# A conditioning shift summed from columns alone, six of its sixteen tiles by GpSimd and ScalarE

## The chip, the cores and the metric

The kernel runs on one core of one Trainium2 chip. The metric is the device time of one execution in microseconds. A core has five engines with a queue each, worked off in order: TensorE (PE in the profile; PEld is its weight load), VectorE (DVE), ScalarE (ACT), GpSimd (POOL) and SyncE (SP), which here only issues DMAs. Engines wait for one another through semaphores.

## The reference, cut to what matters

Two layers; each has a token mixer (a convolution module in layer 0, attention in layer 1) and then a gated network with a width-3 convolution. Every sub-layer takes its shift, scale and gate from one conditioning vector `c`:

```python
def ada_ln(c, w, b):
    mod = jax.nn.silu(c) @ w + b
    shift, scale, gate = jnp.split(mod, 3, axis=-1)
    return shift[:, None, :], scale[:, None, :], gate[:, None, :]
...
        shift, scale, gate = ada_ln(c, ffn_mod_w[i], ffn_mod_b[i])
        h = rms_norm(x, ffn_norm_g[i]) * (1.0 + scale) + shift
        x = x + gate * conv_ffn(h, ffn_up_w[i], ffn_dw_w[i], ffn_dw_b[i], ffn_down_w[i])
```

The width is 2048, the sequence 256, the network's inner width 5632. The case is about `shift` of the first network (`ffn0`): 2048 sums of 2048 products, 16 MB of weights that are read once.

## The kernel before, in words

Activations lie transposed: 16 tiles `x` of 128 channels by 256 tokens. A weight matrix is streamed in pieces of 128x1024, eight 128x128 blocks each. Except in the first product, a piece is split into two parts for exact fp32 products: ScalarE casts it to `wh` (L243), VectorE subtracts to get `wl` (L247), and TensorE multiplies both. There are four buffers of `wh` and of `wl`, six of the loaded `raw`.

A conditioning sum can be made in two ways.

- **By rows, on TensorE** (`mod_rows`, L591): 128x2048 of the weights, four matmuls of 128x512 with the conditioning vector as the stationary side. Four such steps make 512 channels; the result is turned into columns by small matmuls (L607), and a bias is added (L613).
- **By columns, on VectorE** (`mod_reduce`, L338): the transposed weights of 128 channels, 128x2048, are multiplied with the conditioning vector `csr` (a copy in each partition) and summed in one instruction, in place; L342 adds the bias at the end.

For `ffn0` the scale is made by rows (16 steps). Of the shift, `ROWS = 2` groups of 512 channels are made by rows (8 steps), and the other eight tiles by columns.

The place is the second product of the convolution module, called `pw2` here: 16 output tiles, 256 blocks, 32 pieces of weights. Its first eight output tiles are made together (L304 to L306), the last eight one after the other, two pieces each (L298, L299). Each output tile is taken out of PSUM by ScalarE (L978) and VectorE (L979, for the last eight also L981) into `x`; then ScalarE squares it (L406), GpSimd adds the square to `sumsq` (L410), and ScalarE and VectorE make the raw input of the next product (L462, L463). When the shift is complete, its two parts are written beside that input (L473, L474). After `pw2` comes the network's first up-projection, `up00a`.

Work that is not tied to a place stands in `fill`; `tick` takes one step of it after each piece of weights. `mods0` is the generator that makes the rows and the columns of `ffn0`. The framework then orders each engine's instructions; in `mods0`, `behind` keeps a sum behind the instruction that was the engine's last when it was written.

Of the kernel before, what the change touches and what calls it, by code (L numbers as in the profile page):

```python
# [10 lines left out]
F32 = mybir.dt.float32  # L11
F32R = mybir.dt.float32r
AF = mybir.ActivationFunctionType
ALU = mybir.AluOpType
PSUM = bass.MemoryType.PSUM

P = 128
# [14 lines left out]
M0 = 6  # L32
MORE_ROWS = 4
SPLIT_ROWS = 3
ROWS = 2

ROWS_AT = {**{c: (11,) for c in (2, 4, 6, 8, 10, 12)}, 13: (16, 17), 14: (8, 12, 16), 15: (2, 13, 15, 17)}
ROWS_TAIL = 5
# [2 lines left out]
         "o": (0.45, -3.0), "up00a": (0.0, 0.0), "qk0a": (0.0, 0.0),  # L41
         "up00b": (0.28, 0.0), "up10a": (0.0, 0.0), "up10b": (0.25, -2.0), "v0": (0.0, 0.0), "qk0b": (0.42, -1.5)}
QUIET = 6
PRIORITY = 100
MORE_MODS = 2

# [12 lines left out]
class Cfg:  # L59
    def __init__(self, D, T, H, F, CW, FW):  # L60
# [3 lines left out]
        self.GH = 4  # L64
        self.rows0 = min(ROWS, KD // 4)

# [52 lines left out]
def hybrid_trunk(ctx: ExitStack, tc: tile.TileContext, cfg: Cfg, io: dict):  # L119
    nc = tc.nc  # L120
    D, T, H = cfg.D, cfg.T, cfg.H
    KD, KF, CW, FW = cfg.KD, cfg.KF, cfg.CW, cfg.FW
# [34 lines left out]
    csr = const.tile([P, D], F32, name="csr")  # L157
# [10 lines left out]
    def pc(name, i0=0, n=None):  # L168
        if name in cfg.ccols:
            t, (a, b) = cpar["t"], cfg.ccols[name]  # L170
        else:
            t, (a, b) = par, cfg.cols[name]
        return t[:, a:b] if n is None else t[:, a + i0:a + i0 + n]
# [32 lines left out]
    def last_of(engine):  # L206
        return next(ins for ins in reversed(list(nc.cur_bb.bb.instructions)) if ins.engine == engine)

    def behind(ins):

        tc.add_manual_dep(list(nc.cur_bb.bb.instructions)[-1], ins.name,
                          mybir.DependencyInfo(mybir.DependencyClass.NoSync, mybir.DependencyReason.DATA),
                          reason="behind")

    def drain(gens):
        while gens:
            advance(gens, 1)
# [6 lines left out]
    def load(src, dst):  # L224
        tc.keep_in_program_order(nc.sync.dma_start(dst, src))
# [44 lines left out]
    def gemm(name, xh, xl, done, after=None, width=None, halves=0, ready=None, quiet=0,  # L270
# [10 lines left out]
        for blocks, wh, wl in pieces(name):  # L281
            for b, (nb, kt) in enumerate(blocks):
# [25 lines left out]
                if left[nb] == 0:  # L308
                    with tc.high_priority(offset=PRIORITY):
                        done(nb, ps[nb])  # L310
# [7 lines left out]
    mt_at = {"mix0": list(range(2 * KD)), "ffn0": list(range(4 * cfg.rows0, KD)) + list(range(2 * KD, 3 * KD))}  # L318
# [4 lines left out]
    macc = const.tile([P, 3 * KD], F32, name="macc")  # L323
    moda, have, shift_ready = {}, set(), {}

    def mod_load(m, nb, own=False, pool=None):

        v = (pool or mpool).tile([P, D], F32, name="mraw")
        src = io["mt_" + m][mt_at[m].index(nb) if m in mt_at else nb]
        if own:  # L330
            nc.gpsimd.dma_start(v, src)  # L331
        else:
            load(src, v)
        return v

    def mod_reduce(m, nb, v):

        nc.vector.tensor_tensor_reduce(out=v, in0=v, in1=csr, scale=1.0, scalar=0.0, op0=ALU.mult, op1=ALU.add,  # L338
                                       accum_out=macc[:, nb:nb + 1])

    def mod_sum(m, nb, n):
        nc.vector.tensor_tensor(modv[m][:, nb:nb + n], macc[:, nb:nb + n], pc(bname[m], nb, n), op=ALU.add)  # L342
# [37 lines left out]
    def halved(pool, kind, name):  # L380

        low, size, ahead = PAIRS[kind]
        at = ahead if foremost.setdefault(kind, name) == name else 0
        v = pool.tile([P, at + size], F32R, name=name)
        v = bass.AP(tensor=v.tensor, offset=v.offset + at, ap=[list(v.ap[0]), [low, 2], [1, T]])
        return v[:, 0], v[:, 1], v
# [31 lines left out]
    def act_tables(name):  # L418
        tc.keep_in_program_order(nc.scalar.preload_act_table_set(name))
# [25 lines left out]
    class Entry:  # L445
# [31 lines left out]
        def product(self, name, done, table=None):  # L477
# [4 lines left out]
            def after():  # L482
# [6 lines left out]
                if self.rs is not None:  # L489
                    free = KD if i * PB >= n else min(i * PB // FIRST, max(0, KD - STAGGER))  # L490
                    with tc.high_priority(offset=PRIORITY if i * PB >= n else 0):
                        for kt in range(len(self.h), free):
# [17 lines left out]
    with ExitStack() as cv:  # L510
        cpool = cv.enter_context(tc.tile_pool(name="conv", bufs=1))
# [34 lines left out]
        row_tiles, nrow = [], {"n": 0, "near": sum(map(len, ROWS_AT.values())) + ROWS_TAIL, "bias": False}  # L546
# [73 lines left out]
                yield  # L620

        def mods0():
            first = 4 * cfg.rows0
            todo, loaded = list(range(first, KD)), []

            def reduce_loaded():
                while loaded:
                    on = last_of(nc.vector.engine)
                    mod_reduce("ffn0", *loaded.pop(0))
                    behind(on)  # L630

            def load_one():
                nb = todo.pop(0)
                loaded.append((nb, mod_load("ffn0", nb)))

            for _ in mod_rows():
                reduce_loaded()
                yield
                if ("ffn0", 1) in have and todo:
                    load_one()  # L640
                    yield
            while todo:
                load_one()
                yield
                reduce_loaded()
            reduce_loaded()
            if first < KD:
                mod_sum("ffn0", first, KD - first)
            have.add(("ffn0", 0))
            yield  # L650

        gb = cpool.tile([P, KD], F32, name="gb")
        ready = {"k": 0}
        ys = [cpool.tile([P, T], F32, name=f"y{j}") for j in range(KD)]
        for kt in range(KD):
            nc.gpsimd.tensor_tensor(ys[kt], xs[kt], rs, op=ALU.mult)
        htiles = [h_tiles(kt) for kt in range(KD)]
# [165 lines left out]
        for i in range(KD * HEAD // PB):  # L823
            pw1_piece(next(pw1))
            if (i + 1) % (HEAD // PB) == 0:
                start_tile()
        fill.append(mods0())
        load_rows(1)
        look["load"], look["split"] = 5, 0
# [24 lines left out]
        for c in range(KD + 1):  # L854
# [6 lines left out]
            if c > 0:  # L861
                old = [(c - 1, k) for k in vector_taps(c - 1)[split(c - 1):]]
                n = max(len(taps), len(old))
                pad = lambda v: v + [None] * (n - len(v))
                taps = [t for pair in zip(pad(taps), pad(old)) for t in pair if t]
            made = 0
            for s in range(nd):
# [10 lines left out]
                if c == 0 and s % 2 == 1 and 2 + s // 2 < NH:  # L878
                    j = 2 + s // 2
# [112 lines left out]
    def ffn(i, entry, out):  # L992
# [3 lines left out]
        with ExitStack() as fs:  # L996
# [34 lines left out]
            def down_done(h):  # L1031
                def done(nb, ps):
                    if nb < KD - 2:
                        t = t256()
                        nc.scalar.activation(t, ps[:, T:2 * T], AF.Copy, scale=gate(m, nb))  # L1035
                        nc.gpsimd.tensor_tensor(xs[nb], xs[nb], t, op=ALU.add)  # L1036
                    elif nb not in LAST:
                        nc.vector.scalar_tensor_tensor(xs[nb], ps[:, T:2 * T], gate(m, nb), xs[nb],
                                                       op0=ALU.mult, op1=ALU.add)
                    nc.vector.scalar_tensor_tensor(xs[nb], ps[:, :T], gate(m, nb), xs[nb],  # L1040
                                                   op0=ALU.mult, op1=ALU.add)
                    if h == 1 and i == 0:
                        out.add(nb)
                    elif h == 1:
                        out.add(xs[nb])
                        nc.scalar.activation(xs[nb], xs[nb], AF.Copy, scale=pc("fin_g", nb, 1))
                return done
# [9 lines left out]
            act_tables("sqrt_and_others")  # L1057
            gemm(f"down{i}1", gh, gl, down_done(1), quiet=QUIET, both=gb, apart=LAST)
            drain(fill)
# [41 lines left out]
    with ExitStack() as at:  # L1101
# [12 lines left out]
        def attention(h):  # L1114
# [21 lines left out]
            yield  # L1136
            with tc.high_priority(offset=PRIORITY):
                nc.scalar.copy(mh, mk)
# [20 lines left out]
            oh[h], ol[h], ob[h] = halved(apool, "o", f"o{h}")  # L1159
            with tc.high_priority(offset=PRIORITY):  # L1160
                nc.scalar.copy(oh[h], op[:, :T])
# [64 lines left out]
        act_tables("sqrt_and_others")  # L1226
        gemm("o", oh, ol, o_done, ready=lambda kt: oh[kt] is not None, quiet=QUIET, both=ob)

# [11 lines left out]
    for h in range(2):  # L1240
        t = slice(h * HT, (h + 1) * HT)
        nc.vector.reciprocal(rs[:, t], std[:, t])
        v = mpool.tile([P, D], F32, name="mraw")[:, :KD * HT].rearrange("p (k t) -> p k t", k=KD)
# [105 lines left out]
def build(nc, cfg, arrays):  # L1349
    io = {k: nc.dram_tensor(f"in_{k}", v.shape, F32, kind="ExternalInput").ap() for k, v in arrays.items()}  # L1350
    io["out"] = nc.dram_tensor("out_0", (cfg.KD // 2, P, 2 * cfg.T), F32, kind="ExternalOutput").ap()
    with tile.TileContext(nc) as tc:
        hybrid_trunk(tc, cfg, io)
# [19 lines left out]
```

## Time and profile before

| | |
|---|---|
| median of 3 runs | 2252.18 us (2250.47 to 2254.69) |
| the profiled execution | 2246.79 us, its span 2245.1 us |
| PE busy | 2213.9 us, 99% |
| DVE busy | 1811.5 us, 81% |
| ACT busy | 1243.0 us, 55% |
| POOL busy | 417.9 us, 19% |
| DMA | 602.98 MB, mean 269 GB/s |

In rows of the profile, `out<-in` are the program's names, L338 a line of the program, xN a count; behind the bar stand busy time and mean duration, then the idle time of that engine just before these instructions and what ended it. In a timeline the first two columns are start and duration in microseconds.

### The profile page before, as it was taken

The page shows a single profiled execution, that of the slowest core. Times are in us where ns is not written, and L with a number is a line of the kernel's source. Part 1 is how long each engine was busy: PE and PEld are TensorE (multiplying, and loading weights), DVE is VectorE, ACT ScalarE, POOL GpSimd, SP SyncE. Part 2 cuts the span into 40 slices and gives each one's busy share as a digit, 9 for nine tenths or more (in the row PEclk, how much of TensorE's full clock was granted, in tenths as well). Part 3 has the DMA queues.
Part 4 walks back from the last instruction along what each step waited for, and adds up shares of the span by engine and source line. Part 5 has one row for each costly group of instructions (what it writes and reads, how often), then busy time and mean ns, then how long its engine had stood idle before and what let it go on. Part 6 is the DMA issues. An engine that isn't in the chain of part 4 may idle for free.

```text
span 2245.1 us, 35029 instructions
## 1 busy us (share of the span) xinstructions
PE 2213.9 (99%) x12994; PEld 1924.3 (86%) x12994; DVE 1811.5 (81%) x2606; ACT 1243.0 (55%) x2014; POOL 417.9 (19%) x535
## 2 busy tenths in 40 slices
PE   7999999999999999999999999999999999999997
PEld 5887677988888988888898888889888889888887
DVE  7689968989997799998876878899899755777654
ACT  2055655765554455565565555657655544655553
POOL 5058702200002100002311312222000010000031
PEclk9999999999999999999999999999999999999999
DMA  9988698778878977887656788676788656656653
GB/s 398 422 335 310 265 370 338 299 259 300 306 289 291 322 285 289 317 302 268 225 185 249 287 298 296 245 263 234 250 290 289 198 192 194 194 192 191 197 194 113
DMA packets 139134, 602.98 MB, mean 269 GB/s; under 512 B 15441, under 2 KB 15569, under 8 KB 115153
## 3 DMA queue, kind: packets, MB, share of 16 engines
q1 hardware_dynamic: 120242, 464.42, 58.3%
q0 software_dynamic: 18720, 136.32, 16.3%
q8 instruction: 102, 1.67, 0.3%
q14 instruction: 70, 0.57, 0.1%
HBM read 598.58 MB, written 2.10 MB: 268 GB/s over the span
## 4 chain that ended last, share of the span: by engine, by line
PE 87%; DVE 6%; DMA 4%; issue 2%; ACT 1%; POOL 0%; DVEq 0%; SPq 0%; ACTq 0%; POOLq 0%
PE ps L298 46%; PE ps L299 23%; PE ps L700 5%; DMA mraw<-in_mt_mix 3%; DVE mraw L338 2%; PE ps L304 2%; PE ps L306 2%; PE ps L305 1%; DVE wl L247 1%; PE ps L1198 1%; PE ps L1197 1%; PE ps L1196 1%; PE ps L591 1%; PE auxa L591 1%; DVE h L463 1%
## 5 line engine op out<-in xcount | busy, mean ns | idle before, releaser
L298 PE MATMUL ps<-h,wh 128*128 128x512 f32 x3072 | 1048.9, 390 | 0.0
L247 DVE TENSOR_TENSOR wl<-raw,wh 128x1024 fp32r<-128x1024 f32 x688 | 843.7, 1233 | 226.8 <-ACT wh L243 226.3
L243 ACT CAST wh<-raw 128x1024 fp32r<-128x1024 f32 x688 | 719.8, 1049 | 540.0 <-PE ps L298 323.1
L299 PE MATMUL ps<-h,wl 128*128 128x256 f32 x3072 | 848.3, 276 | 0.0
L298 PEld LDWEIGHTS ps<-h,wh 128*128 128x128 f32 x3072 | 576.7, 188 | 119.6
L299 PEld LDWEIGHTS ps<-h,wl 128*128 128x128 f32 x3072 | 576.7, 188 | 0.2
L298 PE MATMUL ps<-g,wh 128*128 128x512 f32 x1320 | 449.0, 389 | 0.0
L338 DVE CUSTOM_DVE_ANT_0 mraw<-mraw,csr 128x2048 f32<-128x2048 f32 x152 | 348.8, 2295 | 27.5 <-DMA mraw<-in_mt_mix 26.9
L299 PE MATMUL ps<-g,wl 128*128 128x256 f32 x1320 | 364.3, 276 | 0.0
L298 PEld LDWEIGHTS ps<-g,wh 128*128 128x128 f32 x1320 | 247.7, 188 | 51.3
L299 PEld LDWEIGHTS ps<-g,wl 128*128 128x128 f32 x1320 | 247.7, 188 | 0.0
L1014 DVE SCALAR_TENSOR_TENSOR t<-t,par 128x254 f32<-128x254 f32 x352 | 169.2, 481 | 60.6 <-ACT t L1011 55.9
L700 PE MATMUL ps<-h,raw 128*128 128x256 f32 x832 | 188.6, 381 | 0.0
L700 PEld LDWEIGHTS ps<-h,raw 128*128 128x128 f32 x832 | 157.8, 191 | 28.3 <-issue 5.8
L1011 ACT ACTIVATE t<-t,par 128x256 f32<-128x256 f32 x176 | 105.6, 600 | 132.3 <-DVE t L1008 132.1
L1036 POOL TENSOR_TENSOR x<-x,t 128x256 f32<-128x256 f32 x56 | 61.1, 1092 | 542.8 <-ACT t L1035 542.8
L740 DVE SCALAR_TENSOR_TENSOR auxb<-u,cpar,auxb 128x256 f32<-128x256 f32 x297 | 121.6, 482 | 4.5 <-ACT auxb L724 3.8
L875 POOL TENSOR_TENSOR y<-y,h 128x256 f32<-128x256 f32 x143 | 104.4, 730 | 13.4 <-ACT h L749 3.3
L331 POOL DMA_DIRECT2D mraw<-in_mt_ffn x64 | 34.5, 540 | 359.9 <-DVE t L1008 247.8
L410 POOL TENSOR_TENSOR sumsq<-sumsq,t 128x256 f32<-128x256 f32 x56 | 62.0, 1107 | 143.7 <-ACT t L406 143.6
L298 PE MATMUL ps<-o,wh 128*128 128x512 f32 x256 | 88.1, 391 | 0.0
L331 POOL DMA_DIRECT2D mraw<-in_mt_mix x48 | 25.9, 541 | 323.5 <-DVE t L1008 169.8
(259 smaller groups left out, 2525.2 us busy)
## 6 DMA issues: line engine op xcount, KB each, us to landing
raw<-in_w_down SPq DMA_DIRECT2D x176, 512.0 KB, 4.3
mraw<-in_mt_ffn POOLq DMA_DIRECT2D x64, 1024.0 KB, 5.9
raw<-in_w_pw SPq DMA_DIRECT2D x96, 512.0 KB, 7.8
mraw<-in_mt_mix POOLq DMA_DIRECT2D x48, 1024.0 KB, 5.5
raw<-in_w_up01b SPq DMA_DIRECT2D x84, 512.0 KB, 5.1
raw<-in_w_up11b SPq DMA_DIRECT2D x84, 512.0 KB, 3.7
raw<-in_w_up00b SPq DMA_DIRECT2D x80, 512.0 KB, 5.0
raw<-in_w_up10b SPq DMA_DIRECT2D x80, 512.0 KB, 4.9
```

The source lines that it names most:

```text
L243: nc.scalar.copy(wh[:, :n], v[:, :n])
L247: nc.vector.tensor_tensor(wl[:, :n], v[:, :n], wh[:, :n].bitcast(F32), op=ALU.subtract)
L298: nc.tensor.matmul(o, wh[:, c], both[kt], start=first, stop=False, skip_group_check=True)
L299: nc.tensor.matmul(o[:, :T], wl[:, c], xh[kt], start=False, stop=left[nb] == 0, skip_group_check=True)
L338: nc.vector.tensor_tensor_reduce(out=v, in0=v, in1=csr, scale=1.0, scalar=0.0, op0=ALU.mult, op1=ALU.add, accum_out=macc[:, nb:nb + 1])
L410: engine.tensor_tensor(self.sum, self.sum, sq, op=ALU.add)
L700: nc.tensor.matmul(banks[j][:, nb // KD * T:(nb // KD + 1) * T], w[:, b * P:(b + 1) * P], hf[kt], start=first, stop=left[j] == 0, skip_gro ...
L740: nc.vector.scalar_tensor_tensor(conv_ps[j], us[j % UBUFS][:, k:k + T], tap(j, k), conv_ps[j], op0=ALU.mult, op1=ALU.add)
L875: nc.gpsimd.tensor_tensor(ys[c], ys[c], pr, op=ALU.add)
L1011: nc.scalar.activation(y, ps[:, :T], AF.Identity, bias=pc(f"fdb{i}", nb, 1), scale=w(FW - 1))
L1014: nc.vector.scalar_tensor_tensor(y[:, s:], ps[:, :T - s], w(k), y[:, s:], op0=ALU.mult, op1=ALU.add)
L1036: nc.gpsimd.tensor_tensor(xs[nb], xs[nb], t, op=ALU.add)
```

## The change

All 16 tiles of the shift are summed from columns; the eight row steps, their copy, turn and bias go. The ten tiles 1, 3, 5, 7, 9, 11 and 12 to 15 are summed by VectorE as before (L338, now L339). The six tiles 0, 2, 4, 6, 8, 10 are loaded into the place of the convolution's result `y`, 16 tiles of 128x256 that are now one tile `yall` and give two buffers of 128x2048; GpSimd multiplies them with `csr` in place (L643), and three steps later ScalarE copies them onto themselves with an accumulated sum into `macc` (L657). Their loads come from SyncE's queue. The columns start when all rows have been loaded, one tile a step. Outside this the line numbers of the changed kernel are one higher up to `mods0` and 28 higher behind it (L981 is L1009).

```diff
-ROWS = 2
+ROWS = 0
+POOL_SUMS, POOL_LAG = 6, 3
...
         def mods0():
-            first = 4 * cfg.rows0
-            todo, loaded = list(range(first, KD)), []
+            todo, loaded, made = list(range(KD)), [], []
+            def on_pool(nb):
+                return nb % 2 == 0 and nb < POOL_SUMS * 2
             def load_one():
                 nb = todo.pop(0)
-                loaded.append((nb, mod_load("ffn0", nb)))
+                if on_pool(nb):
+                    v = yall[:, nb // 2 % 2 * D:(nb // 2 % 2 + 1) * D]
+                    load(io["mt_ffn0"][mt_at["ffn0"].index(nb)], v)
+                else:
+                    v = mod_load("ffn0", nb)
+                loaded.append((nb, v))
+            def sum_loaded():
+                while loaded:
+                    nb, v = loaded.pop(0)
+                    if on_pool(nb):
+                        on = last_of(nc.gpsimd.engine)
+                        nc.gpsimd.tensor_tensor(v, v, csr, op=ALU.mult)
+                        behind(on)
+                        made.append([nb, v, POOL_LAG])
+                    else:
+                        on = last_of(nc.vector.engine)
+                        mod_reduce("ffn0", nb, v)
+                        behind(on)
+            def add_up(now=False):
+                for w in made:
+                    w[2] -= 1
+                while made and (now or made[0][2] <= 0):
+                    nb, v, _ = made.pop(0)
+                    on = last_of(nc.scalar.engine)
+                    nc.scalar.activation(v, v, AF.Copy, accum_out=macc[:, nb:nb + 1])
+                    behind(on)
+            def step():
+                add_up()
+                sum_loaded()
+                if todo:
+                    load_one()
             for _ in mod_rows():
-                reduce_loaded()
                 yield
-                if ("ffn0", 1) in have and todo:
-                    load_one()
+                if nrow["n"] >= 8 * KD // 4:
+                    step()
                     yield
-            while todo:
-                load_one()
+            while todo or loaded:
+                step()
                 yield
-                reduce_loaded()
-            reduce_loaded()
-            if first < KD:
-                mod_sum("ffn0", first, KD - first)
+            add_up(True)
+            mod_sum("ffn0", 0, KD)
...
-        ys = [cpool.tile([P, T], F32, name=f"y{j}") for j in range(KD)]
+        yall = cpool.tile([P, KD * T], F32, name="y")
+        ys = [yall[:, j * T:(j + 1) * T] for j in range(KD)]
```

GpSimd's queue in the second half of `pw2`, before: loads of rows (L571) between the sums of squares.

```order
L571 DMA zrow<-in_mr_ffn 128x2048 x2
L410 TENSOR_TENSOR sumsq<-sumsq,t 128x256 x2
L571 DMA mraw<-in_mr_ffn 128x2048
L410 TENSOR_TENSOR sumsq<-sumsq,t 128x256 x2
L571 DMA zrow<-in_mr_ffn 128x2048
L410 TENSOR_TENSOR sumsq<-sumsq,t 128x256 x3
L571 DMA mraw<-in_mr_ffn 128x2048
L410 TENSOR_TENSOR sumsq<-sumsq,t 128x256
L571 DMA zrow<-in_mr_ffn 128x2048
L410 TENSOR_TENSOR sumsq<-sumsq,t 128x256 x2
L571 DMA mraw<-in_mr_ffn 128x2048
L410 TENSOR_TENSOR sumsq<-sumsq,t 128x256 x4
```

The same place in the changed kernel, from the second of the six products to the end of the sums of squares.

```order
L643 TENSOR_TENSOR y<-y,csr 128x2048
L411 TENSOR_TENSOR sumsq<-sumsq,t 128x256 x4
L643 TENSOR_TENSOR y<-y,csr 128x2048
L411 TENSOR_TENSOR sumsq<-sumsq,t 128x256 x2
L643 TENSOR_TENSOR y<-y,csr 128x2048
L411 TENSOR_TENSOR sumsq<-sumsq,t 128x256
L643 TENSOR_TENSOR y<-y,csr 128x2048
L411 TENSOR_TENSOR sumsq<-sumsq,t 128x256
L643 TENSOR_TENSOR y<-y,csr 128x2048
L411 TENSOR_TENSOR sumsq<-sumsq,t 128x256 x3
```

A DMA issue has become a product over 128x2048; the first product stands ahead of all sums of squares, the second three sums later, and the last four between the seventh sum and the eleventh.

VectorE's queue around output tiles 10 to 12, before (`wl` is a split, `macc` a column sum, `x` and `h` the taking out of a tile; the number behind `h` is the tile).

```order
L338 ISA mraw_2944,macc_104<-mraw_2944,csr_93 128x2048
L338 ISA macc_104 128x1
L979 TENSOR_TENSOR x_92<-x_92,t_3032 128x256
L247 TENSOR_TENSOR wl_3013<-raw_2946,wh_3012 128x1024
L981 SCALAR_TENSOR_TENSOR x_92<-ps_2991,v_mix0_100,x_92 128x256
L247 TENSOR_TENSOR wl_3052<-raw_2985,wh_3051 128x1024
L463 SCALAR_TENSOR_TENSOR h10_3039<-x_92,a_ffn0_2667,h10_3039 128x256
L979 TENSOR_TENSOR x_92<-x_92,t_3096 128x256
L338 ISA mraw_3008,macc_104<-mraw_3008,csr_93 128x2048
L338 ISA macc_104 128x1
L981 SCALAR_TENSOR_TENSOR x_92<-ps_3055,v_mix0_100,x_92 128x256
L247 TENSOR_TENSOR wl_3077<-raw_3010,wh_3076 128x1024
```

And in the changed kernel, tiles 12 and 13.

```order
L1007 TENSOR_TENSOR x_92<-x_92,t_3128 128x256
L1009 SCALAR_TENSOR_TENSOR x_92<-ps_3085,v_mix0_100,x_92 128x256
L339 ISA mraw_3015,macc_104<-mraw_3015,csr_93 128x2048
L339 ISA macc_104 128x1
L464 SCALAR_TENSOR_TENSOR h12_3135<-x_92,a_ffn0_2652,h12_3135 128x256
L248 TENSOR_TENSOR wl_3082<-raw_3017,wh_3081 128x1024
L339 ISA mraw_3042,macc_104<-mraw_3042,csr_93 128x2048
L339 ISA macc_104 128x1
L248 TENSOR_TENSOR wl_3109<-raw_3044,wh_3108 128x1024
L1007 TENSOR_TENSOR x_92<-x_92,t_3187 128x256
L1009 SCALAR_TENSOR_TENSOR x_92<-ps_3147,v_mix0_100,x_92 128x256
L339 ISA mraw_3077,macc_104<-mraw_3077,csr_93 128x2048
```

A column sum now stands ahead of most splits. From the scale's bias (L613) to the sixteenth split behind it, which is the last of `pw2`, the queue holds 10 column sums in place of 7, 15 of L979 and L463 in place of 14, and 7 of L981 in place of 6; the last column sum, which came behind that split, is now ahead of it.

More of the change, by code (lines that the diff above doesn't have):

```diff
@@ L622, in mods0 @@
         def mods0():
-            first = 4 * cfg.rows0
-            todo, loaded = list(range(first, KD)), []
[L626 to L630, printed above, removed]
+            todo, loaded, made = list(range(KD)), [], []
+            def on_pool(nb):
+                return nb % 2 == 0 and nb < POOL_SUMS * 2
             def load_one():
                 nb = todo.pop(0)
-                loaded.append((nb, mod_load("ffn0", nb)))
+                if on_pool(nb):
[4 more added lines that the diff above has]
+                loaded.append((nb, v))
```

## The prediction

> **What bounds the kernel now.** I read the page's busy shares and the chain that ended last, then the stage that the change touches.
>
> ```profile
> PE 2213.9 (99%) x12994; PEld 1924.3 (86%) x12994; DVE 1811.5 (81%) x2606; ACT 1243.0 (55%) x2014; POOL 417.9 (19%) x535
> PE 87%; DVE 6%; DMA 4%; issue 2%; ACT 1%; POOL 0%; DVEq 0%; SPq 0%; ACTq 0%; POOLq 0%
> ```
>
> TensorE is the bound as an average, so work taken from it looks like time gained. The stage tells more. Busy time by engine, from the moment the scale is ready (335.4 us) to the end of VectorE's last split for `pw2`, and to the end of `pw2`; below, what PE waited for in it:
>
> ```profile
> core 0: us, PE busy (x) PEld busy (x) DVE busy (x) ACT busy (x) POOL busy (x), PEclk, DMA share, GB/s
> 335.40:397.85 62.45, 60.79 (x385) 46.69 (x385) 51.55 (x66) 34.34 (x59) 14.84 (x19) 1.00 0.88 346
> 335.40:404.30 68.90, 67.24 (x422) 52.32 (x422) 58.00 (x80) 39.21 (x72) 17.14 (x20) 1.00 0.86 339
> ...
> PE ps L299 <- DVE wl L247: 1.3, 1, 1.3
> PE ps L304 <- ACT t L978: 0.4, 1, 0.4
> ```
>
> PE is never long without work, but DVE is busy for 51.6 of 62.5 us, and the one longer wait of PE is for a split. The last split and the end of the stage (L298, L299 are `pw2`, L304 on `h` is `up00a`):
>
> ```profile
> 396.60 1.21 DVE L247 TENSOR_TENSOR wl<-raw,wh 128x1024 fp32r<-128x1024 f32 x1
> ...
> 403.24 0.40 PE L298 MATMUL ps<-z,wh 128*128 128x512 f32 x1
> ...
> 403.59 0.40 PE L298 MATMUL ps<-z,wh 128*128 128x512 f32 x1
> 403.82 0.28 PE L299 MATMUL ps<-z,wl 128*128 128x256 f32 x1
> 403.94 0.28 PE L304 MATMUL ps<-h,wh 128*128 128x258 f32 x1
> ```
>
> A block takes PE 0.35 us, a piece of eight 2.8 us. The last piece starts at 403.94 - 2.8 = 401.1, its split ends at 397.8: VectorE is 3.3 us ahead, little more than one piece. That small lead is what I argue from.
>
> **What TensorE is spared.** The row steps of this stage and one of them among the blocks, then the turn:
>
> ```profile
> L591 PE MATMUL auxa<-zrow,hot 128*32 128x512 f32 x32 | 4.3, 605 | 0.0
> L591 PE MATMUL auxa<-mraw,hot 128*32 128x512 f32 x32 | 4.3, 604 | 0.0
> ...
> 382.02 0.28 PE L299 MATMUL ps<-z,wl 128*128 128x256 f32 x1
> 382.23 1.07 PE L591 MATMUL auxa<-zrow,hot 128*32 128x512 f32 x8
> 383.23 0.50 PE L298 MATMUL ps<-z,wh 128*128 128x512 f32 x1
> 383.56 0.28 PE L299 MATMUL ps<-z,wl 128*128 128x256 f32 x1
> ...
> 394.43 0.28 PE L299 MATMUL ps<-z,wl 128*128 128x256 f32 x1
> 394.55 0.95 PE L607 MATMUL auxb<-cst,rows 128*128 128x2 f32 x8
> 395.35 0.48 PE L298 MATMUL ps<-z,wh 128*128 128x512 f32 x1
> 395.67 0.28 PE L299 MATMUL ps<-z,wl 128*128 128x256 f32 x1
> ```
>
> A step is eight records, so 64 records are the eight removed steps, all here. From one L299 to the next it is 1.54 us with a step between and 0.35 without: 1.2 us each, 9.6 for eight. The turn costs 1.24 - 0.35 = 0.9. PE alone would end the stage 10.5 us earlier. The eight loads stay 1 MB each; they go from GpSimd's queue to SyncE's, ahead of the weights behind them. As many bytes move, and the DMA engines' share of the stage is 0.88, so I put the loads at 0, between -1 and +3.
>
> **What VectorE gets.** Its groups from 335.4 to 397.85:
>
> ```profile
> L247 DVE TENSOR_TENSOR wl<-raw,wh 128x1024 fp32r<-128x1024 f32 x16 | 19.4, 1215 | 2.3 <-ACT wh L243 2.3
> L338 DVE CUSTOM_DVE_ANT_0 mraw<-mraw,csr 128x2048 f32<-128x2048 f32 x7 | 16.0, 2280 | 0.7 <-DMA mraw<-in_mt_ffn 0.7
> L463 DVE SCALAR_TENSOR_TENSOR h<-x,a_ffn,h 128x256 fp32r<-128x256 f32 x14 | 11.2, 803 | 6.8 <-ACT h L462 6.8
> L979 DVE TENSOR_TENSOR x<-x,t 128x256 f32<-128x256 f32 x14 | 5.8, 415 | 1.0 <-ACT t L978 1.0
> L981 DVE SCALAR_TENSOR_TENSOR x<-ps,v_mix,x 128x256 f32<-128x256 f32 x6 | 2.8, 472 | 0.0
> ```
>
> By the changed order, ahead of the last split there are three more column sums (3 x 2.3 = 6.9) and one more L463, L979 and L981 (0.80 + 0.42 + 0.47 = 1.7): 51.55 + 8.6 = 60.1 us of work, against 57 us that PE has left (67.2 - 10.5). So even with GpSimd's products for nothing, VectorE is the bound of the changed stage, and PE's saving cannot come out whole.
>
> **What GpSimd's products cost VectorE.** No 128x2048 product on GpSimd stands in the trace. Its 128x256 ones do: beside the convolution's taps (L875 beside L740), beside column sums (L656, 21 to 49 us: min/median/max, then both engines' groups), and beside splits.
>
> ```profile
> L875 POOL TENSOR_TENSOR y<-y,h 128x256 f32<-128x256 f32 x143 | 104.4, 730 | 13.4 <-ACT h L749 3.3
> L740 DVE SCALAR_TENSOR_TENSOR auxb<-u,cpar,auxb 128x256 f32<-128x256 f32 x297 | 121.6, 482 | 4.5 <-ACT auxb L724 3.8
> ...
> L656 POOL TENSOR_TENSOR y<-x,rstd x16: 717/1716/2842, 21.3 to 46.1; 128x256 f32<-128x256 f32 x16
> ...
> L338 DVE CUSTOM_DVE_ANT_0 mraw<-mraw,csr 128x2048 f32<-128x2048 f32 x8 | 19.2, 2395 | 1.4 <-DMA mraw<-in_mt_mix 1.4
> L656 POOL TENSOR_TENSOR y<-x,rstd 128x256 f32<-128x256 f32 x16 | 27.6, 1760 | 19.5 <-DVE v_mix L342 19.5
> ...
> 360.13 1.22 DVE L247 TENSOR_TENSOR wl<-raw,wh 128x1024 fp32r<-128x1024 f32 x1
> 361.27 0.96 DVE L463 SCALAR_TENSOR_TENSOR h<-x,a_ffn,h 128x256 fp32r<-128x256 f32 x1
> ...
> 360.87 1.07 POOL L410 TENSOR_TENSOR sumsq<-sumsq,t 128x256 f32<-128x256 f32 x1 [2.71 <-ACT t L406]
> ```
>
> The two take turns. L656 lasts 0.72 us at least and up to 2.84, one column sum longer. L410 at 360.87 gets on when the split ends (361.35), and L463, 0.48 us when alone, then lasts 0.96: it stood behind GpSimd for 0.48. L875 and L740 keep 0.73 and 0.48 us beside one another; L740 has one operand in PSUM (`auxb`). So I take it that the turns concern instructions with two operands in SBUF: the split, the column sum, L979 and L463; L981 reads one from PSUM. The price of 2048 columns: in the 27.6 us of L656, column sums took 8 x 2.28 = 18.2, which leaves 9.4 us for 16 x 256 columns, 4.7 us for 2048. Ends: 8 x 0.48 = 3.8 below, 8 x 0.73 = 5.8 above. I take 4.7, which comes from as many columns in bulk.
>
> [...]
>
> The first product stands ahead of all sums of squares and its load waits for little, so it runs before 340, where DVE has room:
>
> ```profile
> 320.00:340.00 20.00, 20.00 (x162) 15.23 (x160) 9.78 (x18) 11.70 (x18) 1.06 (x2) 1.00 1.01 417
> ```
>
> I count it as 0 (4.7 if it comes late). Five are left: 5 x 4.7 = 23.5 us in which VectorE's two-operand work stands.
>
> **ScalarE** gets six sums over 128x2048. The nearest row:
>
> ```profile
> L243 ACT CAST wh<-raw 128x1024 fp32r<-128x1024 f32 x688 | 719.8, 1049 | 540.0 <-PE ps L298 323.1 <-issue 125.2 <-PE ps L305 26.2
> ```
>
> Twice the columns, 2.1 us each, 12.6 in all, beside 39.2 busy of 68.9 us: hidden as long as GpSimd's product is done when its sum comes up in ScalarE's queue. Casts for splits are queued behind it.
>
> **The sum.** Idle time of VectorE was 62.45 - 51.55 = 10.9 us. Late as it then is, it no longer waits for casts or loads; the waits of L463 for L462 stay at the places where the order has nothing between (7 of 8, 6 us), and I let half of that pass under a product: 3. So the last split ends at 335.4 + 60.1 + 3 + 23.5 = 422.0, and PE's last piece at 424.8, against 403.9: +20.9. Behind it VectorE has one column sum less; PE did not wait there, so I give back 1 at most. That makes +20 us for this execution (2246.8; the median of the runs is 5.4 higher), and I carry it to the median: 2252.2 + 20 = **2272 us**. The unknowns (3.8 to 5.8 a product, idle 0 to 6, the first product 0 or 4.7) give this case +12 to +31: 2264 to 2283.
>
> **The rivals.**
> - *The products fall into VectorE's gaps* (the other side). VectorE's work without any turn-taking is 60.1 less 14 x 0.32 for overlong L463s, 55.6, and with 3 us idle the split chain ends at 394.0, the stage at 396.8: -7, 2245. It needs products that cost VectorE under 3 us in sum, so nearly all of them inside its waits. For it: GpSimd did wait rather than push in where splits follow one another closely:
>
> ```profile
> 402.16 2.35 DVE L247 TENSOR_TENSOR wl<-raw,wh 128x1024 fp32r<-128x1024 f32 x2
> 404.43 0.96 DVE L463 SCALAR_TENSOR_TENSOR h<-x,a_ffn,h 128x256 fp32r<-128x256 f32 x1
> ...
> 402.55 2.56 POOL L410 TENSOR_TENSOR sumsq<-sumsq,t 128x256 f32<-128x256 f32 x1 [4.14 <-ACT t L406]
> ```
>
>  Against it: the waits were 10.9 us in all, none over 1.0, and a product once begun takes 4.7. Chance 0.16.
> - *Part is covered*: one to three of the five products cost their time, the others run while the four split buffers keep PE going. +2 (one) to +11 (three): 2254 to 2263. Chance 0.18.
> - *The products come late and hold up ScalarE.* L410 at 402.55 waited out two splits. The last four products stand one or two sums of squares apart; a late one stops ScalarE at its sum, and the cast (1.0) and the split (1.2) behind it follow in series: some 3 us more in each of four tiles, +12 on the forecast, 2284. [...] Chance 0.18.
>
> **How the numbers follow.** The forecast has 0.48. A measurement of this kernel tells about 0.2% (4.5 us) from no change. Faster by more: most of the first rival, 0.13. Within: its rest (0.03) and the half of the second with one uncovered product (0.10), 0.13. Slower: 0.74. The range from 2249 to 2290 leaves out the first rival (some 0.14) and the upper end of the third (0.06).
>
> **What would show it.** Right: L643 lasts 4 to 7 us; VectorE's L248, L464 or L339 beside it last up to 5 us longer than alone; PE waits for `wl` by 20 us or more between 350 and 425; the stage ends near 425. Wrong: L248 and L339 keep 1.2 and 2.3 us beside L643, or the stage ends before 404. I would be most wrong if the products find their time in waits that I take to be too short.

## The result, and the profile after

The changed kernel takes 2292.0 us (median of 4 runs, 2291.6 to 2292.5) against 2252.3 us before on the same chip: 1.0177 times as long, with a 95% interval from 1.0163 to 1.0192. That is 39.7 us more; 20 were forecast.

Columns, as in the prediction, are PE, PEld, DVE, ACT, POOL busy, granted TensorE clock, DMA share, GB/s. The stage `pw2` of the changed kernel, from the moment the scale is ready to the first block of `up00a`, then to the end of VectorE's last split for `pw2`:

```profile
335.40:448.00 112.60, 75.08 (x351) 61.70 (x352) 86.29 (x95) 50.92 (x93) 42.18 (x19) 0.80 0.54 209
335.40:443.40 108.00, 70.54 (x333) 57.73 (x333) 82.03 (x78) 47.46 (x85) 42.18 (x19) 0.81 0.54 211
```

It takes 112.6 us in place of 68.9. The forecast's sum goes to the last split: 60.1 + 23.5 = 83.6 us of work for VectorE. Up to there it worked for 82.0 us (82.03 in the second line, third column). So its work came out nearly as worked out, and its idle time, 26.0 us where 3 were taken, did not. The end of the stage on TensorE, some 43.7 us later than the 403.94 of before:

```profile
447.56 0.28 PE L300 MATMUL ps<-z,wl 128*128 128x256 f32 x1
447.67 0.28 PE L305 MATMUL ps<-h,wh 128*128 128x258 f32 x1
```

What the engines waited for around it (total, times, longest, in us): PE, then ScalarE, VectorE and SyncE's queue.

```profile
PE ps L300 <- DVE wl L248: 24.6, 8, 6.2
PE ps L299 <- ACT wh L244: 11.0, 6, 5.8
...
ACT t L1006 <- PE ps L300: 38.1, 6, 9.3
...
DVE x L1007 <- ACT t L1006: 17.0, 6, 4.6
DVE h L464 <- ACT h L463: 7.0, 7, 1.5
...
SPq L226 <- ACT y L657: 56.6, 3, 32.7
```

**The products.** The six of them as a group, then VectorE's splits and column sums in the same stretch:

```profile
L643 POOL TENSOR_TENSOR y<-y,csr 128x2048 f32<-128x2048 f32 x6 | 28.2, 4694 | 9.0 <-DMA y<-in_mt_ffn 9.0
...
L248 DVE TENSOR_TENSOR wl<-raw,wh 128x1024 fp32r<-128x1024 f32 x20 | 32.6, 1648 | 2.0 <-ACT wh L244 2.0
L339 DVE CUSTOM_DVE_ANT_0 mraw<-mraw,csr 128x2048 f32<-128x2048 f32 x10 | 27.2, 2718 | 0.0
```

A split took 1.2 us in the mean before, a column sum 2.3. How one product looks from GpSimd, then from VectorE, then from PE:

```profile
406.46 4.69 POOL L643 TENSOR_TENSOR y<-y,csr 128x2048 f32<-128x2048 f32 x1
...
402.69 0.43 DVE L1007 TENSOR_TENSOR x<-x,t 128x256 f32<-128x256 f32 x1 [4.62 <-ACT t L1006]
403.22 0.48 DVE L1009 SCALAR_TENSOR_TENSOR x<-ps,v_mix,x 128x256 f32<-128x256 f32 x1
403.62 2.28 DVE L339 CUSTOM_DVE_ANT_0 mraw<-mraw,csr 128x2048 f32<-128x2048 f32 x1
...
405.83 0.95 DVE L464 SCALAR_TENSOR_TENSOR h<-x,a_ffn,h 128x256 fp32r<-128x256 f32 x1
406.70 6.66 DVE L248 TENSOR_TENSOR wl<-raw,wh 128x1024 fp32r<-128x1024 f32 x2
...
412.28 0.58 PE L300 MATMUL ps<-z,wl 128*128 128x256 f32 x1 [6.23 <-DVE wl L248]
```

The two splits, 2.35 us together before, take 6.66 beside the product: VectorE stands for 4.3 us, nearly all of its 4.7, and PE's longest wait for `wl`, 6.2 us, is this one.

**The loads.** GpSimd's first two products, ScalarE around the sums of them, and SyncE's queue:

```profile
327.32 4.73 POOL L643 TENSOR_TENSOR y<-y,csr 128x2048 f32<-128x2048 f32 x1 [8.49 <-DMA y<-in_mt_ffn]
...
349.42 4.81 POOL L643 TENSOR_TENSOR y<-y,csr 128x2048 f32<-128x2048 f32 x1
...
354.60 0.42 ACT L407 ACTIVATE t<-x 128x256 f32<-128x256 f32 x1 [5.70 <-DVE x L1007]
...
356.72 1.90 ACT L657 ACTIVATE y<-y 128x2048 f32<-128x2048 f32 x1
...
359.77 1.91 ACT L657 ACTIVATE y<-y 128x2048 f32<-128x2048 f32 x1
361.57 0.20 ACT L657 ACTIVATION_READ_ACCUMULATOR y<-y 128x1 f32 x1
...
328.59 0.38 SPq L226 DMA_DIRECT2D raw<-in_w_pw  x1
361.79 0.33 SPq L226 DMA_DIRECT2D y<-in_mt_ffn  x1
362.21 0.38 SPq L226 DMA_DIRECT2D raw<-in_w_pw  x1
```

`y` gives two buffers, so the third load into it has to wait until ScalarE is done with what lies there. The first product ended at 332.05, but its sum is placed three steps later among casts and take-outs and runs at 356.72; the second product came up behind three sums of squares, at 349.42, and its sum at 359.77. The load goes out at 361.79, 0.02 us after the end of this second sum (361.57 + 0.20), so it waited for both. Until then SyncE's queue stands at it, and the weights behind it are not issued for 33 us. The windows show what that does:

```profile
340.00:360.00 20.00, 16.56 (x99) 13.66 (x97) 16.41 (x16) 11.31 (x21) 9.39 (x6) 0.95 0.00 1
360.00:380.00 20.00, 9.72 (x37) 7.76 (x37) 17.02 (x15) 11.09 (x18) 12.60 (x6) 0.70 0.87 338
```

In 340 to 360 us the DMA engines moved next to nothing (1 GB/s). The pieces already loaded last till then; in the next window PE is busy half the time. The lead of a few pieces that hid VectorE's waits is gone, and from there each tile runs in series: PE's last block, ScalarE's L1006, VectorE's L1007, L1009, column sum, L464 and splits, PE again.

### The profile page after: what moved, and what is told of

It reads as the page before. It is cut to its first block, busy times and chain, and to the rows that moved or that the text cites. A ratio compares the mean times of both kernels' runs of the same rounds, so it can differ in the third digit from the quotient of the medians.

```text
span 2290.8 us, 34893 instructions
## 1 busy us (share of the span) xinstructions
PE 2224.4 (97%) x12922; PEld 1935.7 (84%) x12922; DVE 1842.0 (80%) x2609; ACT 1254.1 (55%) x2025; POOL 444.0 (19%) x533
## 4 chain that ended last, share of the span: by engine, by line
PE 93%; DVE 4%; ACT 1%; issue 1%; DMA 0%; POOL 0%; SPq 0%; DVEq 0%; ACTq 0%; POOLq 0%
PE ps L299 47%; PE ps L300 24%; PE ps L728 8%; PE ps L305 2%; PE ps L307 2%; PE ps L306 2%; PE auxb L728 1%; DVE wl L248 1%; PE ps L1226 1%; PE ps L1225 1%; PE ps L1224 1%; PE ps L592 1%; PE auxa L728 1%; DVE mraw L339 0%; DVE h L464 0%
## 5 line engine op out<-in xcount | busy, mean ns | idle before, releaser
L248 DVE TENSOR_TENSOR wl<-raw,wh 128x1024 fp32r<-128x1024 f32 x688 | 852.3, 1246 | 223.9 <-ACT wh L244 223.3
L339 DVE CUSTOM_DVE_ANT_0 mraw<-mraw,csr 128x2048 f32<-128x2048 f32 x154 | 358.0, 2325 | 27.3 <-DMA mraw<-in_mt_mix 27.3
L411 POOL TENSOR_TENSOR sumsq<-sumsq,t 128x256 f32<-128x256 f32 x56 | 66.8, 1193 | 174.0 <-ACT t L407 174.0
```

Of the source, the lines that this page charges most:

```text
L248: nc.vector.tensor_tensor(wl[:, :n], v[:, :n], wh[:, :n].bitcast(F32), op=ALU.subtract)
L411: engine.tensor_tensor(self.sum, self.sum, sq, op=ALU.add)
```

## The experiments

Theory: two causes of about equal size. (1) The products hold VectorE's two-operand work, as forecast. (2) The loads into `y` stop SyncE's queue. In the expectations theory A is the first cause alone. Rivals were VectorE's added column sums by themselves, and products that hold up ScalarE. Kernel before in these batches: 2251.6 to 2252.4 us. "Stage end" is the start of the last `wl` block of `pw2` in the profiled execution. For the kernel before, that execution was 5.5 us under the median, and the record does not show whether the 5.5 us lie in this stage.

| | us | ratio to before, 95% | stage end |
|---|---|---|---|
| before | 2252.3 | | 403.8 |
| changed | 2292.0 | 1.0177 (1.0163 to 1.0192) | 447.6 |
| e1 no product | 2269.7 | 1.0073 (1.0048 to 1.0098) | 424.6 |
| e2 before, with products | 2273.7 | 1.0090 (1.0060 to 1.0121) | 428.8 |
| e3 `y` loads on ScalarE's queue | 2273.6 | 1.0089 (1.0064 to 1.0115) | 428.5 |
| e4 all on VectorE | 2261.3 | 1.0038 (1.0027 to 1.0049) | 414.7 |
| e5 = e1 and e3 | 2255.2 | 1.0010 (0.9995 to 1.0025) | 410.5 |
| e6 products in 8 parts | 2277.9 | 1.0119 (1.0104 to 1.0134) | 433.1 |
| e7 GpSimd only writes | 2270.0 | 1.0083 (1.0068 to 1.0098) | 423.0 |
| e8 sum one step later, not three | 2281.6 | 1.0133 (1.0117 to 1.0150) | 439.1 |
| e9 = e6 and e3 | 2282.1 | 1.0137 (1.0124 to 1.0151) | 438.4 |
| e10 one group by rows | 2262.3 | 1.0049 (1.0037 to 1.0062) | 401.3 |
| e11 one group by rows, two products | 2256.3 | 1.0025 (1.0011 to 1.0038) | |

**e1: the changed kernel without the products.** All other engines have the same instructions in the same order.

```diff
-                        on = last_of(nc.gpsimd.engine)
-                        nc.gpsimd.tensor_tensor(v, v, csr, op=ALU.mult)
-                        behind(on)
```

> The changed kernel without GpSimd's six products (their factor csr is left out of six tiles of the shift); loads, ScalarE's sums and the order on every other engine stay. [...] Rival B (SyncE's queue: the weights stand behind loads of y that wait for ScalarE's sums): the waits stay, 2282 to 2292. Rival C (VectorE's queue takes a tile out before it splits the next piece, a loop through PE, ScalarE and VectorE that needs no product): some 4.7 us less in each of four tiles, 2270 to 2278.

Measured: 22.3 us less than the changed kernel, and 17.3 more than before. The first cause alone was to give back at least 25 us, down to 2267 or less. The time, 2269.7 us, is just above that, and just below C's range. Splits and the wait of SyncE in it:

```profile
L248 DVE TENSOR_TENSOR wl<-raw,wh 128x1024 fp32r<-128x1024 f32 x26 | 32.6, 1261 | 6.4 <-ACT wh L244 6.4
...
SPq L226 <- ACT y L654: 43.5, 3, 28.1
```

The splits are nearly at their own length again (1215 ns before), so the 22.3 us are the products. SyncE still waits 28.1 us for ScalarE's sums: something other than the products has to account for the other 17.

**e2: the kernel before, with six products** on a `y` that is not in use, without loads and sums.

```diff
+                if nb < 14:
+                    v = yall[:, nb % 2 * D:(nb % 2 + 1) * D]
+                    on = last_of(nc.gpsimd.engine)
+                    nc.gpsimd.tensor_tensor(v, v, csr, op=ALU.mult)
+                    behind(on)
```

> The kernel before with six GpSimd products of 128x2048 added over the dead convolution result (extra work, the result unchanged); the order on all other engines is that of before. Theory A: VectorE loses 4.7 us a product against a lead of 3.3 us, +20 to +35, 2272 to 2287. Rivals B and C: no new load and no new order, 2250 to 2257.

Measured: +21.3 us, as theory A has it. The products by themselves cost about the same in either kernel. Column sums, 2279 ns before, beside them:

```profile
L638 POOL TENSOR_TENSOR y<-y,csr 128x2048 f32<-128x2048 f32 x6 | 28.5, 4748 | 0.0
...
L338 DVE CUSTOM_DVE_ANT_0 mraw<-mraw,csr 128x2048 f32<-128x2048 f32 x8 | 26.9, 3366 | 0.0
```

**e3: the loads into `y` from ScalarE's queue**, where they stand behind the sums that free the place (the order of other instructions on VectorE and ScalarE moves with it).

```diff
-                    load(io["mt_ffn0"][mt_at["ffn0"].index(nb)], v)
+                    nc.scalar.dma_start(v, io["mt_ffn0"][mt_at["ffn0"].index(nb)])
```

> The changed kernel with the six loads into y issued from ScalarE's queue, so that no weight stands behind them on SyncE. Theory A: the products stay, 2282 to 2292. Rival B: the 33 us in which SyncE waits for ScalarE go, 2265 or less.

Measured: 18.4 us less than the changed kernel: 2273.6 us lies between the two ranges, so neither theory alone accounts for it. No wait of SyncE for `y` is left, and between 340 and 360 us the DMA engines work. The stage as a whole, below:

```profile
340.00:360.00 20.00, 16.97 (x107) 14.38 (x105) 18.22 (x17) 12.37 (x22) 8.96 (x6) 0.95 0.57 213
...
335.40:428.90 93.50, 68.60 (x362) 58.06 (x361) 86.78 (x95) 51.32 (x94) 41.64 (x19) 0.85 0.66 252
```

VectorE has 95 instructions as in the changed kernel and nearly the same work (86.8 us, there 86.3), but idles for 6.7 us instead of 26.3. These 19.6 us are about what the stage gained (19.1, from 447.6 to 428.5).

**e4: all sixteen tiles on VectorE**, nothing on GpSimd, no load into `y`.

```diff
-POOL_SUMS, POOL_LAG = 6, 3
+POOL_SUMS, POOL_LAG = 0, 3
```

> The changed kernel with all 16 column sums on VectorE (POOL_SUMS = 0): no product, no load into y, six more column sums of 2.3 us. Theory A: VectorE has 60.1 + 13.8 us ahead of the last split, stage end 415 instead of 404: 2260 to 2272. Rival B: nothing of SyncE's wait is left, the time of before plus VectorE's work, 2255 to 2265. Rival C: the loop is longer by a column sum in six tiles than without products: 2275 to 2290.

Measured: +8.9 us over before, which A and B both allow and C does not. VectorE has no idle time at all in 360 to 380 us (third column), and PE waits for splits:

```profile
360.00:380.00 20.00, 11.57 (x51) 9.53 (x52) 20.00 (x24) 8.39 (x15) 5.01 (x4) 0.83 0.98 378
...
PE ps L300 <- DVE wl L248: 16.4, 11, 7.5
```

So the work that TensorE is spared does not come out even without products: VectorE bounds the stage as soon as it takes that work over. As a price this is a rival for the remainder of e1 only if e1 gave VectorE the same work; it gave it six column sums less. Beside e3 the result says something else: with all sums on VectorE the kernel is 12.3 us faster than with six products on GpSimd and the loads out of the way. A column sum takes 2.3 us of VectorE; a product on GpSimd, beside two splits, stopped it for 4.3.

**e5: e1 and e3 together.**

> E3 (loads into y from ScalarE's queue) without the six products (six tiles of the shift lack their factor csr); every other engine's order is that of E3. Two causes that add up, the products (22 us, 2292.0 - 2269.7) and SyncE's wait (18 us, 2292.0 - 2273.6): 2292 - 22 - 18 = 2252, 2249 to 2258. If one cause is only the other's trigger, or the queue order costs by itself (rival C), 2262 to 2272.

Measured: 2255.2 us, not told apart from before. The stage:

```profile
335.40:410.90 75.50, 62.10 (x367) 53.01 (x364) 64.97 (x95) 51.21 (x94) 18.70 (x14) 0.93 0.81 312
```

The four kernels make a square. The products cost 22.3 us with the loads on SyncE and 18.4 with them on ScalarE; the queue costs 18.4 with products and 14.5 without. The two causes add up but for 4 us. The work of VectorE tells the same: 65.0 us here, 86.8 in e3, a difference of 21.8 from products that are on another engine. One thing beside the queue differs: in e3 and e5 the scale is ready at 339.4 and 339.9 us instead of 335.4, so the queue may have cost more than these differences show.

**e6: each product as eight of 128x256.** Other engines as in the changed kernel.

```diff
-                        nc.gpsimd.tensor_tensor(v, v, csr, op=ALU.mult)
-                        behind(on)
+                        for q in range(0, D, 256):
+                            nc.gpsimd.tensor_tensor(v[:, q:q + 256], v[:, q:q + 256], csr[:, q:q + 256], op=ALU.mult)
+                            behind(on)
+                            on = last_of(nc.gpsimd.engine)
```

> The changed kernel with each product in 8 instructions of 128x256 in place of one of 128x2048; the order on the other engines stays. [...] If the length of one hold does the harm: VectorE gets between the parts, 2270 to 2280.

Measured: 14.1 us less than the changed kernel.

```profile
L644 POOL TENSOR_TENSOR y<-y,csr 128x256 f32<-128x256 f32 x48 | 51.0, 1096 | 8.4 <-DMA y<-in_mt_ffn 8.4
...
L248 DVE TENSOR_TENSOR wl<-raw,wh 128x1024 fp32r<-128x1024 f32 x23 | 31.6, 1383 | 11.0 <-ACT wh L244 11.0
```

GpSimd is busy for 51.0 us instead of 28.2, since it now waits for VectorE in its turn (a part with no split or column sum beside it, at 366.37, took 0.72 us; the mean is 1.10), and a split takes 1383 ns instead of 1648. ScalarE now waits for products, 13.0 us in all, and the kernel is faster even so. So the length of one hold mattered here, not only the sum.

**e7: GpSimd writes the place instead of multiplying in it.**

```diff
-                        nc.gpsimd.tensor_tensor(v, v, csr, op=ALU.mult)
+                        nc.gpsimd.memset(v, 0.5)
```

> The changed kernel with a GpSimd instruction that only writes 128x2048 (a constant) in place of each product, so that six tiles of the shift are not those of the reference; all other orders stay. If turns concern GpSimd's reads alone, VectorE's L248, L464 and L339 keep 1.2, 0.5 and 2.3 us beside it, and the time is that of E1, 2266 to 2273. [...]

Measured: 2270.0 us, as without any instruction there (2269.7).

```profile
L643 POOL MEMSET y<- 128x2048 f32 x6 | 10.8, 1807 | 12.6 <-DMA y<-in_mt_ffn 12.6
...
L248 DVE TENSOR_TENSOR wl<-raw,wh 128x1024 fp32r<-128x1024 f32 x26 | 32.6, 1261 | 6.0 <-ACT wh L244 6.0
...
378.56 1.81 POOL L643 MEMSET y<- 128x2048 f32 x1
...
378.83 1.21 DVE L248 TENSOR_TENSOR wl<-raw,wh 128x1024 fp32r<-128x1024 f32 x1
```

The last split lies wholly beside a write and keeps its 1.21 us. So VectorE stood for a product, which reads two operands, and not for a write alone: a split took 1648 ns in the mean with six products of 4.7 us, and 1261 with six writes of 1.8 us, as in e1 with neither.

**e8: the sum one step after the product, not three.**

```diff
-POOL_SUMS, POOL_LAG = 6, 3
+POOL_SUMS, POOL_LAG = 6, 1
```

> The changed kernel with ScalarE's sums one step behind the products in place of three (POOL_LAG = 1). SyncE's third load into y waits for the first sum, which then stands 12 instructions earlier in ScalarE's queue: if SyncE's wait of 33 us costs 18, most of it goes, 2274 to 2282. If only the products count, 2287 to 2293; if sums now come up before their products and stop ScalarE's casts, 2293 to 2305.

Measured: 10.4 us less than the changed kernel. SyncE's waits, and the window in which the DMA engines had stood still:

```profile
SPq L226 <- ACT t L407: 25.4, 2, 15.1
...
SPq L226 <- ACT y L657: 21.5, 2, 14.9
...
340.00:360.00 20.00, 16.65 (x112) 14.43 (x110) 16.51 (x16) 12.76 (x22) 8.64 (x5) 0.99 0.45 175
```

The two waits under L407 are waits for sums too: the loads go out at 363.50 and 375.52 us, 0.03 and 0.02 us after a sum's end, and L407 is what stands behind the sum. So SyncE still waits 46.9 us for sums, in place of 56.6, but no longer than 15.1 us at a time in place of 32.7, and the DMA engines move 175 GB/s between 340 and 360 us. The place of the sum is thus a part of the second cause. How large a part stays open: orders on VectorE and ScalarE move with it, and ScalarE now waits 8.0 us for products.

**e9: parts and ScalarE's queue together.**

> The changed kernel with both partial remedies at once: products in eight parts each, and the loads into y issued from ScalarE's queue. Theory (two separate causes, the length of one hold and the stopped SyncE queue): the gains add, 2292.0 - 14.1 - 18.4 = 2259.5, between 2256 and 2264, and no wait of SyncE for ScalarE's sum. Rival 1 (the parts gained only because VectorE stood still anyway behind the stopped loads; with loads flowing they cost what whole products cost): 2270 to 2274, as with the queue alone. Rival 2 (the parts fall into VectorE's gaps altogether once loads flow): 2254 to 2256, as without products.

Measured: 2282.1 us, more than with either alone: none of the three expectations. ScalarE's wait for the product, and the products:

```profile
ACT y L659 <- POOL y L644: 33.4, 5, 9.6
...
L644 POOL TENSOR_TENSOR y<-y,csr 128x256 f32<-128x256 f32 x45 | 52.5, 1202 | 2.5 <-DMA y<-in_mt_ffn 2.5
```

Eight parts of 1.2 us take 9.6 us where one product takes 4.7, so the sum comes up before they are done and ScalarE stands, its casts and the load behind it. This is the prediction's third rival, which the changed kernel itself did not show, and e6 (13.0 us) and e8 (8.0 us) show in part. The order of other instructions differs here too, so how much of the 22.5 us over 2259.5 is this wait stays open.

**e10: the kernel before with `ROWS = 1`**: 12 tiles on VectorE, four row steps.

> The kernel before with one group of 512 channels by rows in place of two: 12 tiles by columns on VectorE, 4 row steps on TensorE, no product on GpSimd, loads as before. Theory (VectorE bounds the stage as soon as it gets more than it sheds): half of what all sixteen on VectorE cost, some +4, 2253 to 2259. Rival (VectorE's lead of 3 us just covers the added sums, so half of TensorE's 10.5 us comes out): 2246 to 2249.

Measured: +10.8 us, outside both. The stage ends earlier (401.3), but then PE waits for the shift itself:

```profile
PE ps L304 <- ACT h L473: 10.5, 1, 10.5
...
417.39 2.29 DVE L338 CUSTOM_DVE_ANT_0 mraw<-mraw,csr 128x2048 f32<-128x2048 f32 x1
...
420.46 0.16 DVE L342 TENSOR_TENSOR v_ffn<-macc,par 128x12 f32<-128x12 f32 x1
```

L473 writes the shift beside the input of `up00a`. The last column sum starts at 417.39, 16 us behind the end of the stage, and only then the bias (L342) and L473 can follow. The stage alone is no measure, then: a sum that comes after it is paid in `up00a`.

**e11: one group by rows, tiles 4 and 6 by GpSimd and ScalarE, ten by VectorE.**

```diff
-ROWS = 0
+ROWS = 1
...
-                return nb % 2 == 0 and nb < POOL_SUMS * 2
+                return nb in (first, first + 2)
```

> One group by rows, and of the twelve other tiles two by GpSimd and ScalarE (tiles 4 and 6), ten by VectorE. Theory: VectorE has two column sums less than with twelve (4.6 us) but stands still for one product or two (4.7 to 9.4 us), and no load into y waits for a sum, as there are two buffers for two: equal to the kernel with twelve on VectorE within +5, 2253 to 2264. Rival (products this early cost nothing): 2246 to 2250.

Measured: 2256.3 us, 0.25% slower than before: inside the theory's range, but 6 us less than with twelve tiles on VectorE. Its profiled execution took 12 us more than its median, so no stage end is given. None of the eleven kernels beats the one before.

## Why the prediction was half right

- *Direction, and that PE's saving is lost*: right. PE's chance to gain 10.5 us was not taken even without products and without SyncE's wait (e5, +2.9), and not with all sums on VectorE (e4, +8.9).
- *The price of a product*, 4.7 us in which VectorE stands, five of them 23.5: right. One took 4.69 us, the first ran before the stage as assumed, and all together cost 22.3 (e1), 21.3 (e2) or 18.4 us (e5 against e3). What stood beside a product of the changed kernel was L1007 (4.85 us at 349.66, 0.41 alone), a column sum (6.66 at 374.70, 2.28 alone), L464 (3.14 at 368.19, 0.48 at 338.16) and splits; L1009, which reads one operand from PSUM, kept its 0.48 us at 366.76, inside a product (366.54 to 371.04).
- *VectorE's work*, 60.1 + 23.5 = 83.6 up to the last split: right, 82.0.
- *"I put the loads at 0, between -1 and +3"*: this is the step that failed. The loads had been weighed by their bytes and by the DMA engines' share, 0.88. That they wait for a buffer, and that everything on SyncE waits behind them, was not counted, although the change moves these loads and has two buffers for six tiles. It cost 14.5 to 18.4 us (e3, e5).
- *"Late as it then is, it no longer waits for casts or loads"*, 3 us of idle time: wrong for the same reason, 26.0 us. With the loads out of SyncE's queue (e3) it is 6.7 us in the whole stage, which ends at 428.5 for 424.8 forecast, and the kernel takes 2273.6 us for 2272.
- *Rival 3*, ScalarE held up by late products: not in the changed kernel, where ScalarE is not shown waiting for L643. What the profile shows instead is SyncE waiting for ScalarE. e9 shows that the rival exists.
- *PE's last piece*, 2.8 us behind the last split: it took 4.2 (443.46 to 447.67), at a mean clock of 0.59, for which the sum had no term.
- *The range*, +12 to +31: the four unknowns add up to +33 at the upper end, not +31. The measured +39.7 lies outside either way.
- Of what was to show it: L643 of 4 to 7 us, longer splits beside it, and over 20 us of waits for `wl` came (4.7; 6.66 for two; 24.6). The end near 425 did not (447.7).

Taken apart by e1 and e5, the 39.7 us are 22.3 for the products, 14.5 for the queue and 2.9 for all else. These add up by the way they are formed; what tests the two causes is e5, forecast at 2252 and measured at 2255.2.

## What to carry to other kernels

When a load is given another buffer and another queue, look at what frees that buffer and where this stands in its engine's order: here the weights behind one such load on SyncE's queue waited with it, and none was issued for 33 us. Cost an instruction moved to GpSimd by the time for which VectorE's work beside it stands still (products did that in e2 and in the changed kernel, writes alone in e7 did not), and compare that with leaving the work on VectorE: here a product of 4.7 us stopped two splits for 4.3, and a column sum on VectorE took 2.3. And where the lead of a feeding engine is a piece or two, expect to pay what it loses nearly in full: the products, 23.5 us by the sum, cost 18.4 to 22.3.

## What the runs showed of the hardware

**TensorE's clock was lower behind a long wait of its own.** Two neighbouring blocks of `pw2` in the changed kernel after the wait of 6.2 us that ended at 412.28, two more 3 us later, and the clock in the window around them (column before the DMA share):

```profile
413.09 0.41 PE L300 MATMUL ps<-z,wl 128*128 128x256 f32 x1
...
413.73 0.41 PE L300 MATMUL ps<-z,wl 128*128 128x256 f32 x1
...
416.26 0.28 PE L300 MATMUL ps<-z,wl 128*128 128x256 f32 x1
...
416.61 0.28 PE L300 MATMUL ps<-z,wl 128*128 128x256 f32 x1
...
400.00:420.00 20.00, 12.93 (x55) 10.47 (x54) 12.95 (x10) 7.16 (x11) 7.72 (x3) 0.77 0.47 183
```

A block first takes 0.64 us, for the 4.0 us from 412.28 to 416.26, at a mean clock of 0.51. From 416.26 on it takes 0.35, at a clock of 1.00 up to 418, as in the kernel before, whose clock was 1.00 in this stage; the mean clock of the window is 0.77. In the stage 43 blocks stand 0.5 to 0.75 us apart, 12.1 us more than at 0.35 each, against 2 blocks before. Where PE stands in series with VectorE that makes a tile longer still (the last piece took 4.2 us in place of 2.8), and the prediction had no term for it. How long a wait lowers the clock, and how much work behind it brings it back, no run shows. None takes the clock away by itself, so its share of the 39.7 us is not separated: it is in both causes (35 slow blocks in e1, 26 in e3, 9 in e5).

**Short holds cost VectorE less than one long one**, 14.1 us in e6, although GpSimd was busy nearly twice as long: a split took 1383 ns there and 1339 in e9 instead of 1648. But e9 shows that the time then turns up with whoever waits for GpSimd.
